# Norms handed over in steps, a first norm per token, and first weights in halves, in a two-layer diffusion backbone

## The chip, the core and the metric

The kernel runs on one core of a Trainium2 chip, as one program. What counts is the device time of an execution in microseconds (us); the profile is one execution. Engines: PE (TensorE, matmuls), DVE (VectorE), ACT (ScalarE), POOL (GpSimd), SP (its queue issues the DMAs here).

## The reference

Two layers work on 256 latent tokens and 256 context tokens of width 1024. Each layer is a half-step SwiGLU FFN, a token mixer (latent attention, pooling and gated linear attention) and a second FFN. Ahead of each of the three stands an RMS norm with a shift and a scale that come from a product of SiLU(c) with w_ada, nine vectors of 1024 a layer, other ones for latent and context tokens:

```
def rmsnorm(x, g):
    y = xf * lax.rsqrt(jnp.mean(xf * xf, axis=-1, keepdims=True) + EPS)
    return (y * g.astype(F32)).astype(x.dtype)
def modulate(x, shift, scale): return x * (1 + scale) + shift
def ffn_half_step(h, g, shift, scale, gate, w1, w3, w2):
    u = modulate(rmsnorm(h, g), shift, scale)
    return h + 0.5 * gate * ((jax.nn.silu(u @ w1) * (u @ w3)) @ w2)
...
    mod = (sc @ w_ada[l] + b_ada[l]).reshape(B, 1, N_MOD, D)
    h = ffn_half_step(h, g_ffn1[l], mod[:, :, 0], mod[:, :, 1], mod[:, :, 2], ...)
    u = modulate(rmsnorm(h, g_mix[l]), mod[:, :, 3], mod[:, :, 4])
    y, yc = token_mixer(u, uc, ...)
    h = h + mod[:, :, 5] * y
    h = ffn_half_step(h, g_ffn2[l], mod[:, :, 6], mod[:, :, 7], mod[:, :, 8], ...)
```

The context tokens go the same way until the mixer of the last layer.

## The kernel before

All activations lie turned, channels on the 128 partitions: h is 8 blocks (k = 0 to 7) of 128 channels by 512 tokens, the latent stream in columns 0 to 255 (stream 0), the context stream in 256 to 511 (stream 1). Every fp32 product is three fp32r products (`mm3`: whi·uhi, whi·ulo, wlo·uhi; lines 219, 220, 221). So each weight tile that a DMA brings to a `raw` buffer (four of them) is split by ACT (whi, L185) and DVE (wlo, L197), and each operand u as well (uhi on ACT, ulo on DVE, L475). `Weights` issues the loads on SP's queue in the order in which the program needs them, as far ahead as the raw buffers and a number of held tiles (`room`) allow. A scheduler sets the order on each engine from the program's order; each engine works its queue in order.

The modulation vectors come from w_ada in chunks of 512 columns. For chunks 0 to 3 of layer 0 (needed by the first norm; order 0, 2, 1, 3) and for two later ones PE makes the product (`ada`, L327), ACT copies it out (adaev), PE turns it (L339), and DVE adds up and adds the bias (mod, am). All other chunks are summed on DVE between other work (adaacc, L358).

The norm (`norm`): as each block of h is grown (h, L501), ACT squares it and DVE adds the square to acc (L448). When all eight blocks are in, PE multiplies acc with a matrix of 1/1024 (ms, L464), ACT makes rstd (Ln, Exp), DVE makes ut = h·am·rstd (L471), ACT uhi and DVE ulo. At the five places where one phase hands over to the next, called H1 (first FFN to mixer, layer 0), H2 (mixer 0 to the second FFN), H3 (to layer 1), H4 (first FFN to mixer, layer 1) and H5 (mixer 1 to the last FFN) below, all this stands between the last product of one phase and the first of the next. The last products are those of blocks 6 and 7, stream by stream: in the FFN `down([6, 7])`, in the mixer `out([6, 7], True)` with the blocks interleaved. The first product of a phase (`dense`) takes stream 0 over all k first and then stream 1. At H2 a chunk of the modulation for layer 0 (`ada_edge`) stands on PE between the norm and the first product.

The start: SP loads the first weights (512 KB), then x and ctx (8 x 256 KB), chunks 0 and 2 (8 x 256 KB each), three weights, chunks 1 and 3. PE turns x into h (32 transposes of 128x128, L283), and 16 squares, 14 additions and two means follow. `dense_first` computes the first six outputs (w1 and w3 of units m = 0, 1, 2) with u as it comes, k = 1 to 6 in pieces of 256 columns; chunks 1 and 3 lie between them. The constants of the mixer are loaded from ACT's queue after that (`setup_rest`).

Of the kernel before, what the change touches and what calls it, by code (L numbers as in the profile page):

```python
# [38 lines left out]
NHALF, NSLOT, ROOM_FFN, ROOM_MIX, RAWS = 4, 71, 20, 20, 4  # L39
ROOM_0, ROOM_1, LAST = 8, 36, 4  # L40
S0, S1, S2 = 7, 3, 3
# [40 lines left out]
class Weights:  # L82
# [11 lines left out]
    def run_ahead(self):  # L94
        while not self.record:
            while self.loaded < len(self.seq) and len(self.raws) + self.held_raw < RAWS:
                t = self.raw.tile([P, 1024], F32, tag="raw", name="raw")
                self.seq[self.loaded][0](t)
                self.raws[self.loaded] = t
                self.loaded += 1  # L100
# [37 lines left out]
class Net:  # L138
    def __init__(self, nc, a, cst, msk, vecs, wa2, out, pools, w):
# [5 lines left out]
        self.have = set()  # L145
        self.after, self.owed, self.on_pe, self.edge = iter(()), 0, False, []
# [45 lines left out]
    def split(self, hi, lo, src, f32hi):  # L192
# [4 lines left out]
        self.nc.vector.tensor_tensor(out=lo, in0=src, in1=f32hi, op=ALU.subtract)  # L197
# [7 lines left out]
    def cols(self, src, k0, nk, c0, n=P):  # L205
# [7 lines left out]
        return self.w.get(load, m, lambda r, hi, lo: self.halves(r, hi, lo, m))  # L213

# [19 lines left out]
    def setup(self):  # L234
# [15 lines left out]
        for j in (0, 2, 1, 3):  # L250
            if j == 1:
                self.w.run_ahead()
            self.early[j] = [self.slot(name="ada") for _ in range(KD)]
            for k, t in enumerate(self.early[j]):
                nc.sync.dma_start(out=t, in_=self.a["w_ada"][0, k * P:(k + 1) * P, j * T:(j + 1) * T])
# [3 lines left out]
        self.h = one.tile([P, KD, T], F32, name="h")  # L259
        self.csil = one.tile([P, KD, 32], F32, name="csil")  # L260
# [18 lines left out]
        self.acc = self.slot(name="acc")  # L279
        for k in range(KD):  # L280
            ps = self.ps()
            for j in range(4):
                nc.tensor.transpose(ps[:, j * P:(j + 1) * P], xin[j][k // 4][:, (k % 4) * P:(k % 4 + 1) * P], self.ident)  # L283
            if k % 2:
                self.act(out=self.h[:, k, :], in_=ps, func=AF.Copy)
            else:
                nc.vector.tensor_copy(self.h[:, k, :], ps)
            for s in range(2):
                self.square(k, s)

    def setup_rest(self):
# [23 lines left out]
    def ada(self, l, j):  # L315
# [4 lines left out]
        if early or self.on_pe:  # L320
# [15 lines left out]
            yield  # L336
# [7 lines left out]
            if early:  # L344
                yield
            return
# [108 lines left out]
    def norm(self, l, i, n):  # L455
# [3 lines left out]
        u = [(self.slot(F32R, "uhi"), self.slot(F32R, "ulo")) for k in range(KD)]  # L459
        rstd = self.slot(name="rstd")  # L460
# [6 lines left out]
        def some(s, c, ks):  # L467
            for k in ks:
                assert {(l, i, k // 4), (l, i + 1, k // 4)} <= self.have
                t, (hi, lo) = self.half("ut"), u[k]  # L470
# [924 lines left out]
```

## Time and profile before

| | |
|---|---|
| median of 3 runs | 2154.8 us (2153.69 to 2155.99) |
| the profiled execution | 2152.27 us, span 2150.5 us, mean granted clock 0.983 |
| PE busy | 2084.2 us (97%), 11388 instructions |
| DVE busy | 1453.7 us (68%) |
| ACT busy | 882.3 us (41%) |
| DMA | 290.43 MB, mean 135 GB/s |

In the rows of a timeline stand the start and the duration in us, the engine and the line of the kernel, the operation, the tile written and the tiles read (buffer numbers left out), the shape and the count, and in brackets the idle time of that engine before it and what ended it. PE's records overlap, so the pace is read from start to start. An fp32 matmul appears as two records. PEclk is the granted clock of PE, 1.00 being full.

### The profile page before, as it was taken

To read this page: it belongs to the slowest core of one execution; us is meant where nothing else is said; L and a number is where in the kernel's file an instruction comes from. 1 tells how busy PE (TensorE), PEld (TensorE's weight loads), DVE (VectorE), ACT (ScalarE), POOL (GpSimd) and SP (SyncE) were. 2 spreads that over 40 slices of the span, in tenths; PEclk is the share of its full clock that TensorE was granted. 3 is DMA by queue.
4 is the path that set the end of the run, shared out by engine and by line. 5 is a ranking of instruction groups with operands and counts; after the bars stand their busy time and mean duration, and the time that the engine had idled before them with its cause. 6 is when DMAs were issued, how large, how long until landed. Compare 5 with 4: busy or idle time off the path is not lost.

```text
span 2150.5 us, 29894 instructions
## 1 busy us (share of the span) xinstructions
PE 2084.2 (97%) x11388; PEld 1752.5 (81%) x11388; DVE 1453.7 (68%) x2870; ACT 882.3 (41%) x1797; POOL 2.0 (0%) x10
## 2 busy tenths in 40 slices
PE   7999999898999999999999989999999998999999
PEld 4888778786777887888888888888888777998997
DVE  4577877867586665666876785767544687666564
ACT  5232223455344555433223342323343656665552
POOL 0000000000000000000000000000000000000000
PEclk9999999999999999999999999999999989999999
DMA  9355554514432223445555453546442332566663
GB/s 318 100 152 157 172 166 134 160 39 127 118 108 69 79 69 98 119 124 152 164 164 161 135 149 102 151 141 186 137 115 59 96 101 80 142 163 192 181 197 127
DMA packets 431071, 290.43 MB, mean 135 GB/s; under 512 B 16464, under 2 KB 386768, under 8 KB 430928
## 3 DMA queue, kind: packets, MB, share of 16 engines
q1 hardware_dynamic: 430016, 287.09, 46.6%
q8 instruction: 89, 1.46, 0.3%
q10 hardware_dynamic: 912, 1.44, 0.2%
q14 instruction: 54, 0.44, 0.1%
HBM read 287.44 MB, written 1.05 MB: 134 GB/s over the span
## 4 chain that ended last, share of the span: by engine, by line
PE 74%; DVE 11%; DMA 9%; ACT 3%; issue 2%; ACTq 0%; SPq 0%; DVEq 0%
PE ps L219 17%; PE ps L220 17%; PE ps L221 17%; DMA raw<-in_ffn_w_dram 9%; PE fill L219 4%; PE fill L221 4%; PE fill L220 4%; DVE wlo L197 4%; DVE adaacc L358 2%; ACT whi L185 2%; PE sc L1031 1%; PE av L1067 1%; PE ada L327 1%; PE pt L1049 1%; PE gv L219 1%
## 5 line engine op out<-in xcount | busy, mean ns | idle before, releaser
L197 DVE TENSOR_TENSOR wlo<-raw,whi 128x512 fp32r<-128x512 f32 (+3 forms) x912 | 531.3, 619 | 290.0 <-ACT whi L185 279.6
L185 ACT ACTIVATE whi<-raw 128x512 fp32r<-128x512 f32 (+3 forms) x912 | 471.9, 568 | 521.5 <-DMA raw<-in_ffn_w_dram 469.8
L219 PE MATMUL ps<-uhi,whi 128*128 128x512 f32 (+1 forms) x1620 | 564.3, 350 | 8.7 <-ACT uhi L185 5.1
L221 PE MATMUL ps<-uhi,wlo 128*128 128x512 f32 (+1 forms) x1620 | 561.8, 348 | 1.1 <-DVE wlo L197 1.1
L220 PE MATMUL ps<-ulo,whi 128*128 128x512 f32 (+1 forms) x1620 | 562.3, 348 | 0.0
L219 PEld LDWEIGHTS ps<-uhi,whi 128*128 128x128 f32 x1620 | 308.0, 191 | 53.7 <-ACT uhi L185 8.7
L221 PEld LDWEIGHTS ps<-uhi,wlo 128*128 128x128 f32 x1620 | 308.8, 191 | 41.3 <-DVE wlo L197 3.6
L220 PEld LDWEIGHTS ps<-ulo,whi 128*128 128x128 f32 x1620 | 309.3, 191 | 37.9 <-DVE ulo L475 0.6
L358 DVE SCALAR_TENSOR_TENSOR adaacc<-raw,csil,adaacc 128x512 f32<-128x512 f32 x420 | 294.6, 744 | 1.6 <-DMA raw<-in_w_ada_dram 0.8
L219 PE MATMUL ps<-hi,whi 128*128 128x512 f32 (+1 forms) x738 | 272.8, 371 | 6.9 <-DVE h L501 5.4
L221 PE MATMUL ps<-hi,wlo 128*128 128x512 f32 (+1 forms) x738 | 272.0, 369 | 0.2 <-DVE wlo L197 0.2
L220 PE MATMUL ps<-lo,whi 128*128 128x512 f32 (+1 forms) x738 | 271.5, 368 | 0.0
L219 PE MATMUL fill<-uhi,whi 128*128 128x512 f32 (+1 forms) x576 | 203.9, 354 | 0.0
L221 PE MATMUL fill<-uhi,wlo 128*128 128x512 f32 (+1 forms) x576 | 195.9, 340 | 0.0
L220 PE MATMUL fill<-ulo,whi 128*128 128x512 f32 (+1 forms) x576 | 195.4, 339 | 0.0
L219 PEld LDWEIGHTS ps<-hi,whi 128*128 128x128 f32 x738 | 141.2, 191 | 29.8 <-DVE h L501 5.8
L221 PEld LDWEIGHTS ps<-hi,wlo 128*128 128x128 f32 x738 | 141.2, 191 | 23.2 <-DVE wlo L197 0.6
L220 PEld LDWEIGHTS ps<-lo,whi 128*128 128x128 f32 x738 | 141.3, 192 | 22.4 <-DVE lo L197 0.2
L570 DVE TENSOR_TENSOR silu<-silu,ps 128x512 f32<-128x512 f32 (+1 forms) x88 | 54.2, 616 | 133.7 <-ACT silu L185 79.3
L185 ACT ACTIVATE silu<-ps 128x512 f32<-128x512 f32 (+1 forms) x88 | 47.4, 539 | 195.4 <-PE ps L221 195.1
L219 PEld LDWEIGHTS fill<-uhi,whi 128*128 128x128 f32 x576 | 109.3, 190 | 21.7 <-issue 10.6
L220 PEld LDWEIGHTS fill<-ulo,whi 128*128 128x128 f32 x576 | 109.4, 190 | 13.5 <-issue 2.4
(265 smaller groups left out, 2192.0 us busy)
## 6 DMA issues: line engine op xcount, KB each, us to landing
raw<-in_ffn_w_dram SPq DMA_DIRECT2D x198, 512.0 KB, 4.4
raw<-in_w_ada_dram SPq DMA_DIRECT2D x128, 512.0 KB, 3.8
raw<-in_w_in_dram SPq DMA_DIRECT2D x86, 512.0 KB, 4.4
raw<-in_ffn_w_dram SPq DMA_DIRECT2D x48, 384.0 KB, 3.9
raw<-in_ffn_w_dram SPq DMA_DIRECT2D x48, 320.0 KB, 3.2
raw<-in_w_branch_dram SPq DMA_DIRECT2D x48, 256.0 KB, 2.9
ada<-in_w_ada_dram SPq DMA_DIRECT2D x32, 256.0 KB, 5.4
raw<-in_w_out_dram SPq DMA_DIRECT2D x16, 512.0 KB, 5.0
```

What stands on the lines that cost most here:

```text
L185: i = self.nc.scalar.activation(**k)
L197: self.nc.vector.tensor_tensor(out=lo, in0=src, in1=f32hi, op=ALU.subtract)
L219: mm(out, wh, xh, start=start, stop=False)
L220: mm(out, wh, xl, start=False, stop=False)
L221: mm(out, wl, xh, start=False, stop=stop)
L327: nc.tensor.matmul(ps[32 * g:32 * g + 32, :], self.csil[:, k, :], r[i], start=(k < 4), stop=(k >= 4))
L358: nc.vector.scalar_tensor_tensor(out=acc[s], in0=r[i], scalar=c, in1=acc[s], op0=ALU.mult, op1=ALU.add)
L570: nc.vector.tensor_tensor(out=s[:, 0:n], in0=s[:, 0:n], in1=p3[:, 0:n], op=ALU.mult)
L1031: nc.tensor.matmul(sc[:, 0:nk], q[h][:, tt * P:(tt + 1) * P], keys[h][:, k0:T], start=True, stop=True)
L1049: nc.tensor.transpose(pt[:, (2 * x + j) * P:(2 * x + j + 1) * P], ps_[j][:, (kt + x) * P:(kt + x + 1) * P], self.ident)
L1067: nc.tensor.matmul(av[0][64 * x:64 * x + 64, s * NL:(s + 1) * NL], v[2 * s + kt][:, (h + x) * 64:(h + x) * 64 + 64], pts[x][kt // 2][:, (k ...
```

## The change

The first norm no longer goes through acc. ACT squares x as it lies (tokens on partitions) and sums along the row in the same pass; DVE scales x by the token's factor (xr), PE turns xr into hr (32 transposes), and `first_norm` makes u from hr with one ACT pass (scale and bias) and two DVE operations. h is turned from x separately (`residual`): blocks 0 to 3 by 16 transposes that PE does ahead of those of xr, with copies on DVE behind the last scaling, blocks 4 to 7 by 16 transposes between chunk 0 and chunk 2. The first weights come in halves of the contraction (`both`: k = 0 to 3 or 4 to 7 of w1 and of w3, two DMAs of 256 KB into one raw buffer). Nothing but x stands ahead of chunks 0 and 2 any more, then follow three halves, chunks 1 and 3, a fourth half, the constants of `setup_rest` (on SP's queue now), and the rest. `dense_first` works the half k = 0 to 3 for all outputs and then the other half, all with 512 columns. While the first two halves are split, the wlo of a half are held back until u has been issued (`seconds`).

At H1 to H4 the norm goes in steps. The mean of stream 0 is issued after block 6 of stream 1, ahead of block 7 of stream 1 (`norm_ahead`); u of stream 0 is issued after the last product, and the mean and u of stream 1 from within the next `dense`, after k = 1 of stream 0 (`then`). In the mixer the last two blocks go one after the other within a stream, as in `down` (`out_last`). rstd becomes a tile of its own, the u tiles are taken one by one, and the slots are 70 instead of 71.

```diff
@@ setup
+                self.w.run_ahead(3)
...
-        self.acc = self.slot(name="acc")
+        for j in range(4):
+            for c in range(2):
+                self.act(out=junk, in_=xin[j][c], func=AF.Square, accum_out=sums[:, 2 * j + c:2 * j + c + 1])
+            f = fac[:, j:j + 1]
+            nc.vector.tensor_tensor(out=f, in0=sums[:, 2 * j:2 * j + 1], in1=sums[:, 2 * j + 1:2 * j + 2], op=ALU.add)
+            self.act(out=f, in_=f, func=AF.Ln, scale=1.0 / D, bias=self.eps[:, 0:1])
+            self.act(out=f, in_=f, func=AF.Exp, scale=-0.5)
+            for c in range(2):
+                normed = nc.vector.tensor_scalar(out=xr[j][c], in0=xin[j][c], scalar1=f, scalar2=None, op0=ALU.mult)
+        self.residual(range(4), [normed])
         for k in range(KD):
+            t = self.slot(name="hr")
             if k % 2:
-                self.act(out=self.h[:, k, :], in_=ps, func=AF.Copy)
+                self.act(out=t, in_=self.turned(xr, k), func=AF.Copy)
             else:
-                nc.vector.tensor_copy(self.h[:, k, :], ps)
+                nc.vector.tensor_copy(t, self.turned(xr, k))
...
@@ norm
+        for s, c in enumerate(streams):
+            mean(c)
             yield u
+            some(s, c, range(KD))
+            yield u
+    def norm_ahead(self, l, i):
+        order = [(l, i) for l in range(DEPTH) for i in (0, 3, 6)]
+        self.ahead = self.norm(*order[order.index((l, i)) + 1], T)
+        next(self.ahead)
+    def norm_go(self, l, i, n):
+        norm = self.ahead
+        if norm is None:
+            norm = self.norm(l, i, n)
+            next(norm)
+        self.ahead = None
+        u = next(norm)
+        return u, lambda: [next(norm) for _ in range(2)] if n == T else None
+    def first_norm(self):
+        for ks in ([0], [1], [2, 3], range(4, KD)):
+            for k in ks:
...
+                    self.act(out=hi[:, c], in_=self.hr[k][:, c], func=AF.Identity, scale=a, bias=b)
+                    nc.vector.tensor_scalar(out=t, in0=self.hr[k][:, c], scalar1=a, scalar2=b, op0=ALU.mult, op1=ALU.add)
+                    nc.vector.tensor_tensor(out=lo[:, c], in0=t, in1=hi[:, c].bitcast(F32), op=ALU.subtract)
+            yield u
@@ dense
+                if then and s == 0 and k == 1:
+                    then()
@@ dense_first
+        for half, groups in ((0, (range(4), range(4, 6))), (1, (range(6),))):
             for g in groups:
+                for k in range(4 * half, 4 * half + 4):
+                    for j in g:
+                        self.mm3(out[j], units[half][j // 2].block(j % 2 * 4 + k % 4), x[k], k == 0, k == KD - 1)
@@ ffn, down
+                    if c.start and k == 6:
+                        self.norm_ahead(l, i)
                     self.grow(o[k], k, l, i + 2, c, half == 1)
@@ mixer
-        u = self.u = next(self.norm(l, 3, T))
+        self.u, rest = self.norm_go(l, 3, T)
+        def out_last(dcs):
+            for c in (slice(0, NL), slice(NL, T)):
+                for dc, unit, p in zip(dcs, us, o):
+                    for k in range(KD):
+                        self.mm3(p[:, c], unit.block(k), (m[k][0][:, c], m[k][1][:, c]), k == 0, k == KD - 1)
+                    if c.start and dc == dcs[0]:
+                        self.norm_ahead(l, 3)
                     self.grow(p, dc, l, 5, c, True)
```

What it moves, in rows of the order in which the built programs issue (row, line, operation, tile written and tiles read, shape, count). PE at the start, before (x_86 and x_87 are the last tile of tokens; adaev is a chunk copied out, ms the mean):

```order
9 L283 MATMUL ps<-cst_72,x_87 128x128 x4
10 L327 MATMUL ada<-ada,csil 32x512 x8
11 L339 MATMUL ada_298<-cst_72,adaev 128x128 x4
12 L464 MATMUL ms<-acc,cst_72 128x256 x2
13 L327 MATMUL ada<-ada,csil 32x512 x8
14 L339 MATMUL ada_342<-cst_72,adaev 128x128 x4
15 L219 MATMUL ps<-uhi,whi 128x512
```

And after, from the last tile of tokens to the first transposes of the second half of h:

```order
5 L325 MATMUL ps<-cst_72,x_86 128x128 x4
6 L325 MATMUL ps<-cst_72,xr 128x128 x32
7 L373 MATMUL ada<-ada,csil 32x512 x8
8 L386 MATMUL ada_327<-cst_72,adaev 128x128 x4
9 L325 MATMUL ps<-cst_72,x_75 128x128
```

The mean is gone from between the chunks; 32 transposes of xr stand ahead of chunk 0, and 16 of x (from row 9 on) ahead of chunk 2. PE at H2, before, from the last product of w_out (hi, lo) to the first of the FFN (uhi, ulo):

```order
3626 L219 MATMUL ps<-hi,whi 128x256
3627 L220 MATMUL ps<-lo,whi 128x256
3628 L221 MATMUL ps<-hi,wlo 128x256
3629 L464 MATMUL ms<-acc,cst_72 128x256 x2
3630 L380 MATMUL ada<-adapart,cst 128x32
3631 L327 MATMUL ada<-raw,csil 32x512 x8
3632 L219 MATMUL ps<-uhi,whi 128x256
```

And after:

```order
3529 L236 MATMUL ps<-hi,whi 128x256
3530 L237 MATMUL ps<-lo,whi 128x256
3531 L238 MATMUL ps<-hi,wlo 128x256
3532 L429 MATMUL ada<-adapart,cst 128x32
3533 L373 MATMUL ada<-raw,csil 32x512 x8
3534 L236 MATMUL ps<-uhi,whi 128x256 x4
3535 L237 MATMUL ps<-ulo,whi 128x256
```

Both means have left this place: that of stream 0 now stands 24 matmuls ahead of the chunk, that of stream 1 24 matmuls behind the first product. DVE at H4, before, from the last grown block (h) to the first u:

```order
1443 L501 SCALAR_TENSOR_TENSOR h<-ps,am_2_176,h 128x256
1444 L448 TENSOR_TENSOR acc<-acc,sq 128x256
1445 L501 SCALAR_TENSOR_TENSOR h<-ps,am_2_176,h 128x256
1446 L448 TENSOR_TENSOR acc<-acc,sq 128x256
1447 L471 SCALAR_TENSOR_TENSOR ut<-h,am_4_177,rstd 128x256 x3
1448 L475 SCALAR_TENSOR_TENSOR ulo<-ut,mod_169,uhi 128x256
```

And after:

```order
1469 L577 SCALAR_TENSOR_TENSOR h<-ps,am_2_178,h 128x256
1470 L497 TENSOR_TENSOR acc<-acc,sq 128x256
1471 L577 SCALAR_TENSOR_TENSOR h<-ps,am_2_178,h 128x256
1472 L522 SCALAR_TENSOR_TENSOR ut<-h,am_4_179,rstd 128x256 x2
1473 L497 TENSOR_TENSOR acc<-acc,sq 128x256
1474 L526 SCALAR_TENSOR_TENSOR ulo<-ut,mod_171,uhi 128x256
```

The first two ut have passed the last addition to acc, and stand behind the last h.

More of the change, by code (lines that the diff above doesn't have):

```diff
@@ L92, in __init__, with run_ahead @@
         self.raws, self.parts = {}, {}
-    def run_ahead(self):
+    def run_ahead(self, raws=RAWS):
         while not self.record:
-            while self.loaded < len(self.seq) and len(self.raws) + self.held_raw < RAWS:
+            while self.loaded < len(self.seq) and len(self.raws) + self.held_raw < raws:
                 t = self.raw.tile([P, 1024], F32, tag="raw", name="raw")
-                self.seq[self.loaded][0](t)
+                loads = self.seq[self.loaded][0](t)
+                if self.net.tc:
+                    for i in loads or ():
+                        self.net.behind(i, [self.net.last])
                 self.raws[self.loaded] = t
@@ L213, in cols, with both, load @@
         return self.w.get(load, m, lambda r, hi, lo: self.halves(r, hi, lo, m))
+    def both(self, srcs, k0, c0):
+        views = [s[k0 * P:(k0 + 4) * P, c0:c0 + P].rearrange("(k p) c -> p k c", p=P) for s in srcs]
+        def load(t):
+            return [self.nc.sync.dma_start(out=t[:, i * T:(i + 1) * T].rearrange("p (k c) -> p k c", k=4), in_=v)
+                    for i, v in enumerate(views)]
+        return self.w.get(load, 2 * T, lambda r, hi, lo: self.halves(r, hi, lo, 2 * T))
     def mm3(self, out, wts, x, start, stop):
@@ L345, in ada @@
                 yield
+                if j in (0, 2):
+                    yield
             return
@@ L458, in norm @@
         streams = [slice(s * NL, (s + 1) * NL) for s in range(n // NL)]
-        u = [(self.slot(F32R, "uhi"), self.slot(F32R, "ulo")) for k in range(KD)]
-        rstd = self.slot(name="rstd")
+        u = [None] * KD
+        rstd = self.rstd
         def mean(c):
@@ L547, in ffn, with rest @@
         ahead = 3 if begin else 2
-        norm = self.norm(l, i, n)
         if begin:
+            norm = self.first_norm()
             self.adas(5)
-            u = next(norm)
+            self.residual(range(4, KD))
+            self.xin = None
             self.adas(5)
-            self.w.room = ROOM_0
-            first = unit(0)
+            part = lambda half, ms: [self.both((w1, w3), 4 * half, m * P) for m in ms]
+            first = [], []
+            for m in (0, 1):
+                self.seconds = []
+                self.w.room = 4 * m + 4
+                first[0].extend(part(0, [m]))
+                u = next(norm)
+                for second in self.seconds:
+                    second()
+            self.seconds = None
             next(norm)
             self.w.room = ROOM_1
-            first += unit(1) + unit(2)
+            first[0].extend(part(0, [2]))
+            first[1].extend(part(1, [0]))
+            def rest():
+                self.adas(1)
+                next(norm)
+                self.w.room = ROOM_2
+                first[1].extend(part(1, [1, 2]))
         else:
```

118 lines of the change are left out of this document (66 added, 52 removed).

## The prediction

> **What bounds the kernel now.** I read the totals first, then TensorE's waits, then the timelines of PE, DVE and ACT at the places the waits point to. The first fence is the page's line of busy times and the first line of TensorE's waits (us in total, times, longest).
>
> ```profile
> PE 2084.2 (97%) x11388; PEld 1752.5 (81%) x11388; DVE 1453.7 (68%) x2870; ACT 882.3 (41%) x1797; POOL 2.0 (0%) x10
> ...
> PE ms L464 <- DVE acc L448: 14.8, 7, 4.3
> ```
>
> TensorE is busy 2084.2 of 2150.5 us, so about 66 us of idle time are all that a change of order can win, apart from time at half clock. The largest wait is the one the change is aimed at: the mean matmul (ms) waits for the sum of squares 7 times, 14.8 us. The next fence is TensorE's timeline over the start (start, duration, operation, then in brackets the idle time and what ended it).
>
> ```profile
> 6.74 5.52 PE L283 MATMUL ps<-cst,x 128*128 128x128 f32 x32
> 12.37 5.71 PE L327 MATMUL ada<-ada,csil 128*32 128x512 f32 x16
> 18.76 0.66 PE L339 MATMUL ada<-cst,adaev 128*128 128x128 f32 x4 [0.69 <-ACT adaev L185]
> 22.30 1.10 PE L464 MATMUL ms<-acc,cst 128*128 128x256 f32 x4 [2.88 <-DVE acc L448]
> 23.33 3.32 PE L327 MATMUL ada<-ada,csil 128*32 128x512 f32 x16
> ...
> 32.05 0.79 PE L219 MATMUL ps<-uhi,whi 128*128 128x512 f32 x1 [3.98 <-ACT uhi L185]
> ...
> 52.67 1.92 PE L327 MATMUL ada<-ada,csil 128*32 128x512 f32 x16
> ...
> 71.02 0.28 PE L220 MATMUL ps<-ulo,whi 128*128 128x256 f32 x1
> 71.26 0.40 PE L219 MATMUL ps<-uhi,whi 128*128 128x512 f32 x1
> ...
> 75.37 0.39 PE L219 MATMUL ps<-uhi,whi 128*128 128x512 f32 x1
> ```
>
> The first dense product starts at 32.05. At 71.26 its last eighteen matmuls begin, one for each unit and product of k=7, and the next unit begins at 75.37: the stage lasts 43.3 us. Eighteen in 4.11 us are 0.228 each at 512 columns; at 256 columns (two from 71.02 to 71.26) they follow each other by 0.12, so two halves cost 0.24.
>
> **The start, step by step.** The new path runs through ACT, DVE and PE in turn. The rows for its steps (L356 has minimum/median/maximum in ns; the row with 206 is a group with its mean in ns):
>
> ```profile
> 7.62 1.28 ACT L181 ACT_TABLE_LOAD   x1
> 588.59 0.77 ACT L185 ACTIVATE p<-sc,mx,scal 128x512 f32<-128x512 f32 x1
> 589.34 0.59 ACT L185 ACTIVATE gqk<-fill 128x512 f32<-128x512 f32 x1
> L185 ACT ACTIVATE orstd<-orstd 128x4 f32<-128x4 f32 x4 | 0.8, 206 | 0.1
> L356 DVE TENSOR_SCALAR adaacc<-raw,csil x60: 477/480/486, 93.9 to 1527.4; 128x512 f32<-128x512 f32 x60
> 11.30 2.48 DVE L287 COPY h<-ps 128x512 f32<-128x512 f32 x4 [4.02 <-PE ps L283]
> 29.90 0.16 DVE L404 SCALAR_TENSOR_TENSOR am<-mod,vec 128x8 f32<-128x8 f32 x1
> 37.52 1.89 DVE L197 TENSOR_TENSOR wlo<-raw,whi 128x512 fp32r<-128x512 f32 x3
> 31.09 1.31 ACT L185 ACTIVATE uhi<-ut,mod 128x256 fp32r<-128x256 f32 x3 [1.66 <-DVE ut L471]
> ```
>
> ACT can begin squaring after its table load, at 8.90. An ACT pass that also sums takes 0.75 from start to the next start (588.59 to 589.34), so eight are 6.0; the eight one-column Ln and Exp at 0.2 are 1.6, a hop to DVE and back 0.3: the last token factor is there at 16.8. DVE then scales the last two tiles (0.4 each) and, in its queue behind them, copies the first half of h (2.5), for which PE's second half of xr transposes waits on its PSUM tiles; with the last transposes 0.6 PE is free at 20.7. Chunk 0 of the modulation comes next: 1.9 at the price of 52.67, since its weights, which paced PE at 12.37 to 18.08, have long landed. Copy out and transposes 1.3 (the gap and row at 18.76), 23.9. Sixteen transposes of x for the second half of h: between 1.5 and 2.8 (5.52/32 each), taken 1.5, 25.4. Chunk 2: 1.9, 27.3; at 23.33 it ran without a DMA wait, and now it runs later while its loads were issued earlier. Out and transposed 1.3, three small DVE operations 0.6, two uhi 1.0: 30.2, and 0.5 more for a part at half clock. First dense product 30.7, against 32.05: only 1.3 us earlier, because a chain of ACT, DVE and PE takes the place of the chain that ended at the mean.
>
> The stage behind it: 144 matmuls at 0.228 are 32.8, and chunks 1 and 3 with their transposes 5.0, so 37.8. Before, the same work with 256-column pieces for k=1 to 6 is 6 x 3 x (2 x 0.228 + 12 x 0.12) = 34.1, plus 5.0, 39.1 of its 43.3; 4.2 went to half clock and to waits for u. Now the halves of u come from DVE: after the first uhi stand, up to the ulo of k=1, two ulo, two wlo, four ut and two ulo more (0.6 each for wlo by 37.52, 0.4 for the others), 4.4 us, against 2.5 of PE work on k=0, a wait of 1.9; with 0.7 of half clock 2.6. The stage ends at 30.7 + 37.8 + 2.6 = 71.1 instead of 75.4: **4.3 us won at the start**. Bounds: all links at half clock (first dense at 34.3, below) leave 0.7, one more wait of 1.9 makes it -1; squares at the price of a plain copy and no loss behind them give 7. The tables moved from ACT's queue to SP's (1.2 MB by their shapes) stand behind chunk 3 and ahead of two halves of weights needed only after 72 matmuls, 16 us into the stage: nothing. Weights in halves: the same bytes; nothing.
>
> **The hand-overs.** H2, mixer 0 to the second FFN, is the dearest. DVE's row, then PE's, then the clock in the window (PEclk is the third number from the end):
>
> ```profile
> 896.46 1.27 DVE L501 SCALAR_TENSOR_TENSOR h<-ps,mod,h 128x256 f32<-128x256 f32 x3 [3.31 <-PE ps L221]
> 896.50 0.28 PE L221 MATMUL ps<-hi,wlo 128*128 128x256 f32 x1
> 898.93 0.67 PE L464 MATMUL ms<-acc,cst 128*128 128x256 f32 x2 [2.15 <-DVE acc L448]
> 900.53 3.30 PE L327 MATMUL ada<-raw,csil 128*32 128x512 f32 x16
> 903.76 0.58 PE L219 MATMUL ps<-uhi,whi 128*128 128x256 f32 x1
> 902.00:904.00 2.00, 2.00 (x13) 0.34 (x6) 1.91 (x7) 1.99 (x4) 0.00 (x0) 0.50 0.22 56
> ```
>
> After the last w_out matmul (896.50) all growing, both sums and both means stand in a row, and the chunk that follows runs at half clock: 3.3 instead of 1.9. Now stream 0's mean is issued before the last quarter of w_out, and PE goes straight from it into that chunk: 896.62 + 0.3 for that mean + 0.2 + 1.9 = 899.0, with u of stream 0 made meanwhile (h 0.4, ut 0.4, uhi 0.5). Stream 1's mean costs 0.3 inside the dense product. Won: 903.76 - 899.3 = **4.5**. Between 2.5 (if the chunk's last weights land 2 us late: they are needed 4 us earlier than now) and 5.
>
> At the other three no chunk on PE covers u. Rows of H1 (421), H3 (1276) and H4 (1644), DVE's and then PE's first product:
>
> ```profile
> 420.96 0.48 DVE L501 SCALAR_TENSOR_TENSOR h<-ps,am,h 128x256 f32<-128x256 f32 x1 [0.44 <-PE ps L221]
> 422.80 1.28 DVE L471 SCALAR_TENSOR_TENSOR ut<-h,am,rstd 128x256 f32<-128x256 f32 x3 [0.39 <-ACT rstd L185]
> 424.19 0.74 PE L219 MATMUL ps<-uhi,whi 128*128 128x256 f32 x4 [0.96 <-ACT uhi L185]
> 1276.20 0.48 DVE L471 SCALAR_TENSOR_TENSOR ut<-h,am,rstd 128x256 f32<-128x256 f32 x1
> 1278.43 0.78 PE L219 MATMUL ps<-uhi,whi 128*128 128x256 f32 x2
> 1644.23 0.48 DVE L501 SCALAR_TENSOR_TENSOR h<-ps,am,h 128x256 f32<-128x256 f32 x1 [2.50 <-PE ps L221]
> 1645.81 1.27 DVE L471 SCALAR_TENSOR_TENSOR ut<-h,am,rstd 128x256 f32<-128x256 f32 x3
> 1646.89 0.74 PE L219 MATMUL ps<-uhi,whi 128*128 128x256 f32 x4 [0.17 <-ACT uhi L185]
> ```
>
> DVE's new order puts ut right behind the last h, but not ahead of it. From ut to the first product go 1.1 us (1645.81 to 1646.89). H4: h at 1644.23 + 0.3 for the early mean, ut 0.4 later, product at 1646.0, and 0.3 for the second mean: 0.6 won. H1: the copy of vec1 lies between, ut at 421.9, product at 423.0, with the second mean 0.9 won. H3: there DVE is behind with weights and modulation sums and the order gives it the same operations ahead of ut plus a small one: ut at 1276.35, product at 1277.45, 0.6 for a mean at half clock: 0.4 won. Together **1.9**, between 0 and 4 (ut first thing after PE stops). H5 is unchanged.
>
> **Sum.** 4.3 + 4.5 + 1.9 = 10.7. The profiled execution took 2152.27 (2150.5 span and 1.8 around it): 2141.6. It lies 2.5 below the median of the runs, 2154.8, so the time to expect is 2144. A difference of 0.2% (4.3 us) is about what can be told from none.
>
> **The rivals.** *The start at half clock.* If the sparse work from 9 to 19 us (only transposes) leaves PE at half clock, chunk 0 and chunk 2 cost 3.3 each and the sixteen transposes 2.8: 4.1 more, of which 0.5 is counted already; first dense at 34.3, and 0.7 is left of the start: 7.1 in all, 2147.7. What decides is whether transposes alone bring the clock up. Two answers on the transposes, from 9 to 10 and from 10 to 11 us (mean ns in the second number behind the bar):
>
> ```profile
> L283 PE MATMUL ps<-cst,x 128*128 128x128 f32 x7 | 1.6, 409 | 0.0
> L283 PE MATMUL ps<-cst,x 128*128 128x128 f32 x11 | 1.5, 292 | 0.0
> ```
>
> They get faster, 409 to 292 ns, after three microseconds in which nothing but transposes had run. That speaks against this rival, but in the new order they come in bursts with gaps. [...] Chance 0.15.
>
> *The hand-overs keep their length.* DVE takes h of the last block, then ut, in order; where it is late (H3) or H2's chunk waits for weights, only the start's 4.3 is left: 2150.5. For it speaks DVE's 68%; against it, that at H4 DVE had been idle 2.5 us when h came. Chance 0.09, half of it within 0.2%.
>
> *Slower: the early mean stalls PE.* It stands in PE's queue ahead of a whole block of 24 or 33 products, and waits for stream 0's sum on DVE. What such a wait costs shows here, a product held up by DVE, and the clock behind it:
>
> ```profile
> 410.02 0.58 PE L219 MATMUL ps<-hi,whi 128*128 128x256 f32 x1 [3.44 <-DVE h L501]
> 416.16 0.32 PE L220 MATMUL ps<-lo,whi 128*128 128x256 f32 x1
> 415.89 0.41 DVE L448 TENSOR_TENSOR acc<-acc,sq 128x256 f32<-128x256 f32 x1
> ```
>
> 3.4 us of wait, then 28 matmuls from 410.02 to 416.16, 0.22 apart instead of 0.12, 2.8 more: 6.2 a place. Two places eat the whole gain and more, four give 24.8 - 10.7 = 14 us more, 2169. The point: it decides where DVE finishes stream 0's sum more than 3 us behind the block k=6 of stream 1. At H1 the sum is done at 416.3, when that block (33 matmuls from 410.02, 28 of them by 416.16) runs to 416.8; at H4 the slack is over 2 us, at H2 about half a microsecond. Chance 0.11, of it 0.09 slower, 0.02 within 0.2%.
>
> **How the numbers follow.** Likeliest, both parts pay: 0.54, 2139.5 to 2148.5, predicted 2144. Half clock at the start 0.15 (2147.7), hand-overs unchanged 0.09 (2150.5), slower 0.11 (2156 to 2169); better than the bounds of the middle, with a start of 7 and hand-overs of 9, 0.08 (2139); no effect at all 0.03. Faster 0.54 + 0.15 + 0.05 + 0.08 = 0.82; within 0.2% 0.04 + 0.02 + 0.03 = 0.09; slower 0.09. A range from 2137 to 2151 leaves out the slower case, the lower half of the better one and the no-effect case: about 0.2.
>
> **What would show it.** Right: the first dense product at 30 to 31.5 and the next unit at 70 to 72; the early means at H1 to H4 without a wait; H2's chunk in 2 us directly behind w_out; TensorE's wait for acc down from 14.8 to under 4. Wrong: a first dense product after 33, or a wait over 1 us in front of an early mean; or a loss in the first FFN behind 75 us, where the order of weights and modulation sums on DVE also moves and where I forecast nothing.

## The result, and the profile after

The changed kernel took 2143.51 us (median of 4, 2142.09 to 2145.75) beside 2155.14 for the kernel before (2153.69 to 2155.99): ratio 0.9948, 95% interval 0.9930 to 0.9965, so 11.2 us faster. The forecast was 2144.0 in a range of 2137 to 2151. The profiled execution took 2143.83, its span is 2141.7, 8.8 less than the span before.

First the page's line of busy times and four lines of TensorE's waits (us in total, times, longest):

```profile
PE 2078.9 (97%) x11308; PEld 1745.6 (82%) x11308; DVE 1452.2 (68%) x2872; ACT 887.3 (41%) x1805; POOL 2.0 (0%) x10
...
PE ps L236 <- ACT uhi L188: 9.8, 4, 4.9
...
PE ps L236 <- DVE h L577: 6.0, 2, 3.4
PE ms L513 <- DVE acc L497: 4.5, 3, 2.7
PE ps L236 <- ACT whi L188: 3.4, 3, 1.9
```

The mean's wait for acc fell from 14.8 us to 4.5, and 2.7 of that is H5, which the change leaves alone. The wait for uhi (9.8) now stands at the head of the list: part of one wait has turned into another. TensorE's timeline of the start shows chunk 0, chunk 2, the first dense product, and the first product of unit m=3:

```profile
19.50 1.92 PE L373 MATMUL ada<-ada,csil 128*32 128x512 f32 x16
...
24.55 1.92 PE L373 MATMUL ada<-ada,csil 128*32 128x512 f32 x16
...
29.73 0.73 PE L236 MATMUL ps<-uhi,whi 128*128 128x512 f32 x2 [1.81 <-ACT uhi L188]
...
71.16 0.39 PE L236 MATMUL ps<-uhi,whi 128*128 128x512 f32 x1
```

Both chunks take 1.92, the price at full clock (the trace's record of the granted clock has 1.00 from 18.00 to 31.65; at half clock, 0.50, a chunk took 3.30 in the kernel before). The dense product starts at 29.73 instead of 32.05, and the stage ends at 71.16 instead of 75.37. H2 on TensorE, from the early mean over the last w_out matmul and the chunk to the first product of the FFN:

```profile
888.81 0.59 PE L513 MATMUL ms<-acc,cst 128*128 128x256 f32 x2
...
891.99 0.28 PE L238 MATMUL ps<-hi,wlo 128*128 128x256 f32 x1
892.11 0.31 PE L429 MATMUL ada<-adapart,cst 128*128 128x32 f32 x2
892.34 2.34 PE L373 MATMUL ada<-raw,csil 128*32 128x512 f32 x16
894.62 0.74 PE L236 MATMUL ps<-uhi,whi 128*128 128x256 f32 x4
```

No row has a bracket, so TensorE waits for nothing here. From the last w_out matmul to the first product go 2.63 us; before they were 7.26 (896.50 to 903.76). The first products of H1, H3 and H4, and of H3 also the early mean and the last product ahead (1264.23):

```profile
419.51 0.74 PE L236 MATMUL ps<-uhi,whi 128*128 128x256 f32 x4 [1.60 <-ACT uhi L188]
...
1259.90 0.67 PE L513 MATMUL ms<-acc,cst 128*128 128x256 f32 x2 [1.35 <-DVE acc L497]
...
1264.23 0.28 PE L238 MATMUL ps<-hi,wlo 128*128 128x256 f32 x1
...
1269.51 1.22 PE L236 MATMUL ps<-uhi,whi 128*128 128x256 f32 x4 [4.85 <-ACT uhi L188]
...
1637.60 0.74 PE L236 MATMUL ps<-uhi,whi 128*128 128x256 f32 x4 [1.51 <-ACT uhi L188]
```

H1 and H4 wait 1.6 and 1.5 us for u; H3 waits 4.85, and its first product then has the long duration of half clock (1.22 against 0.74; the record has 0.50 from 1267.3 to 1274.1).

To place every microsecond I cut the span at marks that each trace has: the first and last silu of each FFN on ACT, the first `msk` matmul of each mixer, and h of block 5 in w_out on DVE. A stage is the time between two marks. Each number below is a difference of start times. "Again" is a second execution of the changed kernel; "start", "hands" and "H2" are the experiments that follow. The kernel before was traced once, in an execution of 2152.27 us of the first group; in the groups of the last four columns its runs had medians of 2148 to 2149. So a difference of a few us between its column and one of these can belong to the execution.

| stage (us) | before | after | again | start | hands | H2 |
|---|---|---|---|---|---|---|
| start, to the first silu | 72.22 | 67.96 | 69.20 | 68.76 | 72.72 | 66.68 |
| first FFN, first to last silu | 282.94 | 283.79 | 279.61 | 278.82 | 283.17 | 279.00 |
| H1, to msk | 94.96 | 94.07 | 94.65 | 93.09 | 94.03 | 93.02 |
| mixer 0, to h of block 5 | 435.42 | 434.79 | 433.49 | 434.21 | 434.28 | 433.82 |
| H2, to the first silu | 40.73 | 36.68 | 36.25 | 39.33 | 36.25 | 36.38 |
| second FFN | 280.78 | 280.84 | 280.85 | 280.85 | 280.84 | 280.84 |
| H3, last silu to first silu | 95.72 | 96.12 | 95.79 | 95.07 | 96.68 | 95.17 |
| first FFN, layer 1 | 279.79 | 279.79 | 279.79 | 279.78 | 279.80 | 279.79 |
| H4, last silu to msk | 84.62 | 84.10 | 84.12 | 86.11 | 84.11 | 86.06 |
| rest of the span | 483.32 | 483.56 | 483.55 | 483.88 | 483.12 | 483.94 |

From before to after: start -4.26, first FFN +0.85, H1 -0.89, mixer -0.63, H2 -4.05, H3 +0.40, H4 -0.52, the rest +0.3: the 8.8 us of the two spans.

### The profile page after: what moved, and what is told of

Its sections match the earlier page's. It is cut to its first block, busy times and chain, and to the rows that moved or that the text cites. A ratio compares the mean times of both kernels' runs of the same rounds, so it can differ in the third digit from the quotient of the medians.

```text
span 2141.7 us, 29782 instructions
## 1 busy us (share of the span) xinstructions
PE 2078.9 (97%) x11308; PEld 1745.6 (82%) x11308; DVE 1452.2 (68%) x2872; ACT 887.3 (41%) x1805; POOL 2.0 (0%) x10
## 4 chain that ended last, share of the span: by engine, by line
PE 74%; DMA 10%; DVE 10%; ACT 4%; issue 2%; ACTq 0%; DVEq 0%; SPq 0%
PE ps L236 17%; PE ps L237 17%; PE ps L238 17%; DMA raw<-in_ffn_w_dram 8%; PE fill L236 4%; PE fill L238 4%; PE fill L237 4%; DVE wlo L200 4%; DVE adaacc L407 2%; ACT whi L188 2%; DMA raw<-in_w_in_dram 1%; PE sc L1138 1%; PE av L1174 1%; PE pt L1156 1%; PE gv L236 1%
## 5 line engine op out<-in xcount | busy, mean ns | idle before, releaser
L200 DVE TENSOR_TENSOR wlo<-raw,whi 128x512 fp32r<-128x512 f32 (+3 forms) x912 | 531.1, 618 | 289.0 <-ACT whi L188 280.3
L236 PE MATMUL ps<-uhi,whi 128*128 128x512 f32 (+1 forms) x1584 | 557.1, 354 | 12.7 <-ACT uhi L188 9.8
L237 PE MATMUL ps<-ulo,whi 128*128 128x512 f32 (+1 forms) x1584 | 556.0, 352 | 0.2 <-DVE ulo L565 0.2
L238 PE MATMUL ps<-uhi,wlo 128*128 128x512 f32 (+1 forms) x1584 | 555.0, 351 | 1.0 <-DVE wlo L200 1.0
L236 PEld LDWEIGHTS ps<-uhi,whi 128*128 128x128 f32 x1584 | 300.2, 190 | 57.8 <-ACT uhi L188 12.2
L238 PEld LDWEIGHTS ps<-uhi,wlo 128*128 128x128 f32 x1584 | 301.2, 190 | 43.0 <-DVE wlo L200 3.6
L237 PEld LDWEIGHTS ps<-ulo,whi 128*128 128x128 f32 x1584 | 301.7, 190 | 39.4 <-DVE ulo L565 0.6
L236 PEld LDWEIGHTS ps<-hi,whi 128*128 128x128 f32 x738 | 139.9, 190 | 31.5 <-DVE h L577 6.4
```

Of the source, the lines that this page charges most:

```text
L200: second = lambda: self.nc.vector.tensor_tensor(out=lo, in0=src, in1=f32hi, op=ALU.subtract)
L236: mm(out, wh, xh, start=start, stop=False)
L237: mm(out, wh, xl, start=False, stop=False)
L238: mm(out, wl, xh, start=False, stop=stop)
```

## The experiments

Each group ran on one chip, beside the kernel before. Microseconds against it are (1 - ratio) times its median in that group (2148.8, 2148.1 and 2148.0). The changed kernel measured in two of these ways: 11.2 us above, 12.0 us in the second group.

**The start alone, and the hand-overs alone.** Does the sum of the parts hold? The first kernel is the changed one with the hand-overs undone, the second the kernel before with the new hand-overs.

```
start alone:                       hand-overs alone:
-  self.norm_ahead(l, i)           +  norm in steps, norm_ahead, norm_go, then, out_last
-  u, later mean and u of stream 1    (first norm, weights and loads as before)
+  u and mean at once; w_out blocks interleaved
```

> The changed kernel with the four hand-overs as before the change (both means and all of u behind the last product, last two w_out blocks interleaved by k); only the start is new. Theory 1 (the parts add, each by its own place): first dense product at 29.7 us, unit m=3 at 71.1, so 4.3 us less than before there, and the whole time 4.3 less than before (ratio 0.998). Theory 2 (the start's gain is given back inside the first FFN, because the weights are no earlier and TensorE meets the same waits and a longer time at half clock): 3 us or less are left at 410 us and at the end (ratio 0.9986 or nearer 1). Hand-overs H1 to H4 as before: waits for acc of about 14.8 less the 2.9 of the start.

> The kernel before the change with the new hand-overs alone (means in steps, u of stream 1 inside the next product, last w_out blocks one after the other); the start is the old one, first dense product at 32.0. Theory 1: 6.4 us less than before (ratio 0.997), of it 4.5 at H2 (the modulation chunk on TensorE in 2 us instead of 3.3, directly behind w_out), 0.9 at H1, 0.4 at H3, 0.6 at H4. Theory 2 (hand-overs carry almost all): 8 us or more (0.9963).

Start alone: 2142.78, ratio 0.9973 (0.9962 to 0.9983), 5.8 us faster. Hand-overs alone: 2141.93, ratio 0.9969 (0.9957 to 0.9981), 6.7 faster. I had 4.3 and 6.4; both lie in the intervals, and their sum, 12.5, is the change's 11.2 to 12.0 within them. The parts add up. TensorE at H2, without the new steps and with them:

```profile
888.27 0.67 PE L513 MATMUL ms<-acc,cst 128*128 128x256 f32 x2 [2.15 <-DVE acc L497]
889.14 0.67 PE L513 MATMUL ms<-acc,cst 128*128 128x256 f32 x2 [0.20 <-DVE acc L497]
...
889.88 1.92 PE L373 MATMUL ada<-raw,csil 128*32 128x512 f32 x16
```

```profile
892.39 0.59 PE L466 MATMUL ms<-acc,cst 128*128 128x256 f32 x2
...
895.93 1.92 PE L329 MATMUL ada<-raw,csil 128*32 128x512 f32 x16
```

The wait of 2.15 for acc is what the steps remove. But the old order's chunk took 1.92 here and 3.30 in the profile before: 1.4 of the 4.05 us that H2 won between the first two traces was half clock that the old order does not always meet. Without it H2 is worth 39.33 - 36.25 = 3.1 us.

**H2 alone.** The changed start and steps at H2 only sizes H1, H3 and H4 by what is missing; the changed kernel ran beside it. The edit, shortened:

```
-  self.norm_ahead(l, i)                     # in the FFN
+  if i in (0, 3): next(norm), next(norm)    # H1, H3, H4: all of the norm at once
```

> The changed start and the steps at H2 alone; H1, H3 and H4 as before. My terms: start 4.3 + H2 4.5 = 8.8 below the kernel before, ratio 0.9959, 1.9 above the change; in the trace H2's chunk directly behind w_out and the first product 2.5 to 2.7 behind the last w_out product. Rival: the hand-overs' gain lies mostly at H1, H3 and H4 (less half clock behind them), then only 4.3 + 2.5 = 6.8, ratio 0.9968.

> The changed kernel once more, beside the others of this group, to size its parts on one chip and to see a second execution. If the parts add up as predicted (start 4.3, hand-overs 6.4), it stands 10.7 us, ratio 0.995, below the kernel before. On the first FFN (first dense product to the first product of block 6, stream 1, at H1; 377 us in the changed kernel's trace, 370 to 372 where the hand-overs were undone or h was turned later): if the difference belongs to the order of the code, it is 377 again here; if it belongs to one execution (when a weight lands, where a half-clock stretch falls), 370 to 374.

H2 alone: 2137.75, ratio 0.9951 (0.9937 to 0.9965), 10.5 us; the changed kernel: 2137.11, ratio 0.9944 (0.9932 to 0.9957), 12.0. So 1.5 us are left for the other three, where I had 1.9, but the intervals overlap by more than that, and the table does not bear it out: H4 is 1.9 us shorter with the steps, H3 0.6 and H1 1.6 longer, in all 0.3 longer. At the old H3 and H4 TensorE waits at the second mean:

```profile
1260.51 0.78 PE L513 MATMUL ms<-acc,cst 128*128 128x256 f32 x2 [4.36 <-DVE acc L497]
...
1628.17 0.67 PE L513 MATMUL ms<-acc,cst 128*128 128x256 f32 x2 [1.42 <-DVE acc L497]
```

At H4 that wait was followed by 3.4 us at half clock (the trace's record of the granted clock has half clock from 1629.6 to 1633.0); with the steps there is none. By my estimate such a stretch of 3.4 us costs up to 1.7 us of work, most of the 1.9: the granted clock is 0.50 in it, and in the kernel before the matmuls of 256 columns follow each other by 0.22 at half clock and by 0.12 at full. At H3 the wait of 4.36 became one of 4.20 for uhi in the second execution of the changed kernel.

The second execution also settles two points. First FFN: 279.6 against 283.8 in the first trace of the same code, so that difference is not the code's. TensorE's waits there, first trace and second:

```profile
288.49 0.50 PE L236 MATMUL ps<-uhi,whi 128*128 128x512 f32 x1 [0.98 <-ACT whi L188]
...
291.69 0.80 PE L236 MATMUL ps<-uhi,whi 128*128 128x512 f32 x1 [1.92 <-ACT whi L188]
```

```profile
288.57 0.50 PE L236 MATMUL ps<-uhi,whi 128*128 128x512 f32 x1 [1.30 <-ACT whi L188]
289.90 0.50 PE L238 MATMUL ps<-uhi,wlo 128*128 128x512 f32 x1 [0.59 <-DVE wlo L200]
```

Weights come late around 288 us, 2.9 against 1.9 us, and 6.8 against 3.4 us of half clock follow. The five other traces with the new start and the same plan of modulation sums (start alone, H2 alone and the next three experiments) show 277.7 to 280.3, the two with the old start 282.9 and 283.2. So the new start may win some 3 us more in this FFN than I counted. That is not shown: both traces with the old start are of long executions (2152.27 us, and 2146.76, the longest of that kernel's six), and no run tests why weights should come earlier.

The other point is the clock at the start. The transposes of xr from 16 to 17 us and from 18.4 to 19.4 us (count, then busy us and mean ns), first trace and second:

```profile
L325 PE MATMUL ps<-cst,xr 128*128 128x128 f32 x7 | 1.7, 418 | 0.0
...
L325 PE MATMUL ps<-cst,xr 128*128 128x128 f32 x11 | 1.4, 278 | 0.0
```

```profile
L325 PE MATMUL ps<-cst,xr 128*128 128x128 f32 x7 | 1.8, 426 | 0.7 <-DVE xr L309 0.7
...
L325 PE MATMUL ps<-cst,xr 128*128 128x128 f32 x7 | 1.7, 422 | 0.0
```

And windows of 2 us (after the window: its length, busy us and instructions of PE, PEld, DVE, ACT, POOL, then PEclk, DMA share, GB/s), first trace and second:

```profile
16.00:18.00 2.00, 2.00 (x11) 1.70 (x10) 2.00 (x5) 1.81 (x3) 0.00 (x0) 1.00 1.05 387
18.00:20.00 2.00, 2.00 (x22) 1.44 (x24) 2.00 (x5) 0.99 (x2) 0.00 (x0) 1.00 1.05 382
```

```profile
16.00:18.00 2.00, 2.00 (x11) 1.70 (x10) 2.00 (x5) 1.81 (x3) 0.00 (x0) 0.50 1.04 382
18.00:20.00 2.00, 2.00 (x11) 2.00 (x10) 2.00 (x4) 0.87 (x2) 0.00 (x0) 0.50 1.06 386
20.00:22.00 2.00, 2.00 (x18) 1.02 (x20) 1.53 (x3) 0.61 (x2) 0.00 (x0) 0.69 1.15 308
```

From 16 to 18 us both traces have 11 instructions of like length (418 and 426 ns), so both run at the half-clock pace, although the first window prints 1.00. That 1.00 is no measurement: the first trace's record of the clock begins at 18.00, with full clock, and what lies ahead of the record is printed as full. In the second trace the record begins at 10.98 with full clock, falls to half at 14.39 and is back at 21.22, behind 5.4 us of transposes without a gap. So in both executions most transposes of xr run at half clock; in the first the full clock comes 3.2 us earlier, and the first dense product at 29.73 instead of 31.33. Of these 1.6 us, 0.3 lie ahead of the last burst of transposes (15.34 and 15.62). The clock falls back in this way in three of the ten traces with this start, which are all but the kernel before, the hand-overs alone and the next experiment (the three are the second execution, start alone and the earlier u): there chunk 0 begins 4.9 to 5.4 us behind the start of that burst, in the other seven 4.2 to 4.3. The rival of the half clock is half true: it holds for most transposes of xr in both executions, but chunks 0 and 2 and the sixteen transposes of x between them ran at full clock (all but the first 0.2 us of chunk 0 in the second execution), and the price between executions is some 1.2 us and not 4.1.

**Turning h later.** All 32 transposes of x between chunks 0 and 2, so that nothing stands ahead of xr on PE.

```
-  self.residual(range(4), [normed])
-  self.residual(range(4, KD))
+  self.residual(range(KD))
```

> The changed kernel with all 32 transposes of x for h (and their copies) between modulation chunks 0 and 2, none ahead of those of xr. Theory 1 (the start is bound by the chain ACT squares, DVE scaling, DVE copies of h, TensorE, chunk 0): chunk 0 starts about 2.2 us earlier (17.3 instead of 19.5), chunk 2 about 1 us earlier, first dense product at 28.7, 1 us less in all. Rival (TensorE at half clock when it does only transposes of xr, with gaps, up to there): chunk 0 takes 3.3 instead of 1.9 us and the first dense product comes at 30 or later, no gain.

2137.29, ratio 0.9943 (0.9930 to 0.9956): the same as the change. Its start on TensorE, with one row of DVE:

```profile
12.59 6.63 PE L324 MATMUL ps<-cst,xr 128*128 128x128 f32 x32 [5.65 <-DVE xr L309]
...
17.48 2.48 DVE L318 COPY hr<-ps 128x512 f32<-128x512 f32 x4 [0.66 <-PE ps L324]
...
22.37 3.66 PE L324 MATMUL ps<-cst,x 128*128 128x128 f32 x32
...
31.14 0.73 PE L236 MATMUL ps<-uhi,whi 128*128 128x512 f32 x2 [1.81 <-ACT uhi L188]
```

PE idles 5.65 us for the first xr, and the transposes of xr end at 19.2 as in the change (19.5). They follow each other without a gap, at 0.21 us each until 18.3 and at 0.11 from there, the pace of the 32 of x at 22.37; this trace's record of the clock begins at 18.28, with full clock. So it is TensorE at half clock that paces them, and DVE, whose copies of h are out of the way, waits 0.66 us for it. Chunk 0 ran at full clock (1.92) all the same: the rival's outcome, no gain, came true, and its reason only for the transposes. The 16 that came off this path then cost 1.75 between the chunks (3.66 against 1.91 for the 16 that the change has there).

**u of the first two blocks earlier still.** u of k=0 and 1, stream 0, ahead of the last h on DVE.

```
-  some(s, c, range(KD))
+  some(s, c, range(2)); yield u     # for stream 0, called ahead of the last h
+  some(s, c, range(2, KD))
```

> The changed kernel, with u of blocks k=0 and 1 of stream 0 made ahead of the last grown block instead of behind it. If the 1.5 to 1.6 us that TensorE still waits for uhi at H1 and H4 (and 4.85 at H3) come from DVE's order (last h, then ut), as theory 1 says, they go: 1.5 less at H1 and at H4, 2 to 3 at H3, in all 5 us less than the changed kernel. Rival: these waits are the latency of the last block itself or DVE being behind with weights and modulation sums; then ut made earlier only pushes weight splits back, and the time stays within 1 us of the changed kernel.

2146.66, ratio 0.9988 (0.9978 to 0.9997): only 2.6 us faster than the kernel before, some 9 slower than the change. Against the second execution H2 grew by 2.4 (38.63), H3 by 1.9 (97.73) and H4 by 3.1 (87.18). TensorE at H2 (chunk) and H4:

```profile
889.87 1.91 PE L373 MATMUL ada<-raw,csil 128*32 128x512 f32 x12
...
895.63 1.05 PE L373 MATMUL ada<-raw,csil 128*32 128x512 f32 x4 [1.15 <-DMA raw<-in_w_ada_dram]
```

```profile
1641.08 0.39 PE L238 MATMUL ps<-uhi,wlo 128*128 128x256 f32 x1 [0.84 <-DVE wlo L200]
1642.69 0.74 PE L236 MATMUL ps<-uhi,whi 128*128 128x256 f32 x4 [0.88 <-ACT uhi L188]
1644.07 0.38 PE L237 MATMUL ps<-ulo,whi 128*128 128x256 f32 x1 [0.64 <-DVE ulo L526]
```

What moves ahead on DVE pushes something back: the chunk's last four matmuls wait for their load, and at H4 wlo, uhi and ulo are late in turn, with 3.4 us of half clock behind them. An earlier u alone is no gain while DVE has the same work to do.

**Two PSUM tiles for a block.** At H1 and H3 TensorE waits for h (6.0 us in two waits) ahead of block 6, stream 1.

```
-  o = {k: self.ps() for k in ks}
+  o = {(k, c.start): self.ps() for k in ks for c in spans}
```

> The change, with a PSUM tile of its own for each stream of blocks 6 and 7 in the FFN (before: one tile for both streams of a block). Theory: block 6 of stream 1 waits for h of block 6, stream 0 (3.40 at H1, 2.57 at H3) only since both lie in one tile; with two tiles that wait is gone, but DVE is as late as ever, so the early mean behind it waits instead (2 to 4 us at H1 and H3): no more than 2 us gained in all, 0 likeliest. Rival: the wait was the loss itself, and 6.0 of wait plus about 3 of half clock behind it are won: 9 us below the change.

2137.82, ratio 0.9949 (0.9936 to 0.9963): no gain. The early means at H1 and H3:

```profile
405.02 1.19 PE L513 MATMUL ms<-acc,cst 128*128 128x256 f32 x2 [5.37 <-DVE acc L497]
...
1253.86 1.19 PE L513 MATMUL ms<-acc,cst 128*128 128x256 f32 x2 [3.90 <-DVE acc L497]
```

The wait for h is gone and stands in front of the mean, as expected. DVE is late, and TensorE waits for the next of its results in its place.

**Taking the modulation sums off DVE there.** DVE's rows at H3 of the changed kernel say what it is late with:

```profile
1266.00 2.07 DVE L407 SCALAR_TENSOR_TENSOR adaacc<-raw,csil,adaacc 128x512 f32<-128x512 f32 x3
1267.98 0.48 DVE L577 SCALAR_TENSOR_TENSOR h<-ps,am,h 128x256 f32<-128x256 f32 x1
...
1268.45 0.46 DVE L522 SCALAR_TENSOR_TENSOR ut<-h,am,rstd 128x256 f32<-128x256 f32 x1
```

The last product of the FFN began at 1264.23, and its h is made at 1267.98, behind three modulation sums. Four kernels move such sums: to the units ahead ("quiet", both FFNs of layer 0), to layer 1 ("quiet1", second FFN only), and simply later ("quiet01", both FFNs), the last ("quiet01_sep") also with two PSUM tiles. From 20 us ahead of the last product of the FFN to 4 us behind it, DVE works 14 such sums at H3 in the change (second execution), and 9, 6 and 0 in the first three kernels; at H1 it works 8 in the change, and none in the first and the third kernel.

```
-  if len(ks) == 1:
+  if len(ks) == 1 and not (half and phase < 2 and ks[0] > 2):   # quiet1: phase == 1
       self.adas(ADA["down"][phase])
-  up=(1.5, 1.25, 1, 0)
+  up=(1.66, 1.4, 1, 0)                                          # the first kernel only
```

> The change, with the modulation sums kept off DVE while the last three single blocks of the first two FFNs' second half and blocks 6 and 7 are grown, and as many more sums per unit ahead (1.66 and 1.4 quarters a unit instead of 1.5 and 1.25). Theory: at H1 and H3 TensorE waits for h, acc and uhi because DVE works modulation sums of 0.67 each between (11 of them from 1252 to 1268); without them the waits of 3.40 (H1) and 2.57 + 1.35 + 4.85 (H3) fall by half or more, and 5 to 8 us are won on the change. Rival: the weights' own splits set DVE there, or the sums cost as much where they go (first FFN at 290 us: whi waits of 2.9 now): no gain, or 2 to 4 us lost.

> The change, with no modulation sums asked for while the last three single blocks of the second FFN of layer 0 are grown; nothing is raised elsewhere, so these sums come later, in layer 1. Theory: what holds TensorE at H3 (2.57 + 1.35 + 4.85 us) is DVE at work on modulation sums between h and acc, and layer 1's first FFN has room for them (its stage lasts 279.8 us in every run so far, without a wait): the stage of H3 (last silu to first silu, 96 us) becomes 90.5 and the time 5 below the change. Rival: the sums cost as much where they go (as in the run where they went into the units ahead, which took 5.1 us there): 0, at most 2 gained.

> As the run before, and the same at the end of the first FFN of layer 0. Theory: the stage of H1 falls from 94.5 to 87, as in the run with raised sums, now without a longer FFN ahead of it, and H3 by 5: 11 to 13 below the change, about 2125. Rival: DVE lacks the time in the mixer or in layer 1 instead, and the stage there grows by what is won: within 3 of the change.

> As the run before, with a PSUM tile of its own for each stream of blocks 6 and 7. Theory: alone this brought nothing, since the early mean then waited 5.37 and 3.90 us for acc; with DVE free of sums acc is in time, and the wait of block 6 for h (6.0 at H3 in the run with raised sums) goes: 2 to 6 below the run before. Rival: DVE is late with the weights' second parts too: 0.

| | median, us | ratio (95%) | first FFN | H1 | mixer 0 | second FFN | H3 | FFN, layer 1 |
|---|---|---|---|---|---|---|---|---|
| the change, again | 2137.11 | 0.9944 (0.9932 to 0.9957) | 279.61 | 94.65 | 433.49 | 280.85 | 95.79 | 279.79 |
| to the units ahead | 2141.24 | 0.9969 (0.9957 to 0.9981) | 289.41 | 86.69 | 435.04 | 285.94 | 90.33 | 279.79 |
| H3 only, to layer 1 | 2129.49 | 0.9918 (0.9905 to 0.9932) | 279.41 | 92.68 | 434.10 | 280.85 | 86.76 | 281.32 |
| both, later | 2128.45 | 0.9911 (0.9897 to 0.9926) | 279.67 | 87.14 | 441.19 | 280.85 | 86.17 | 280.59 |
| both, two tiles | 2131.05 | 0.9917 (0.9903 to 0.9931) | 276.55 | 86.64 | 442.38 | 280.85 | 86.17 | 280.51 |

At H1 and H3 the sums are the cause: without them the stage of H1 shrinks by 7.5 to 8.0, and that of H3 by 5.5, 9.0 and 9.6, the more the fewer are left there. What that is worth hangs on where they go. In the units ahead of H1 and H3 they cost 9.8 and 5.1, about all that this brings; where the sums of H1 come later, mixer 0 grows by 7.7, all of the 7.5 won at H1. It holds no more sums than the change's (54 in both), but they lie elsewhere in it, and this line of TensorE's waits shows what the change's mixer 0 does not have:

```profile
PE pt L1156 <- DVE p L1146: 5.9, 1, 5.9
```

TensorE's clock is at half from 571.0 to 577.8 us around that wait. That the moved sums delay p is likely and not tested. In layer 1 the sums of H3 alone (126 in its first FFN instead of 108) cost 1.5 of 9.0. Two PSUM tiles add nothing. H3 with its sums in layer 1, DVE's rows and TensorE's:

```profile
1252.04 0.48 DVE L577 SCALAR_TENSOR_TENSOR h<-ps,am,h 128x256 f32<-128x256 f32 x1 [2.71 <-PE ps L238]
1252.44 0.87 DVE L522 SCALAR_TENSOR_TENSOR ut<-h,am,rstd 128x256 f32<-128x256 f32 x2
```

```profile
1253.51 0.74 PE L236 MATMUL ps<-uhi,whi 128*128 128x256 f32 x4 [1.51 <-ACT uhi L188]
```

Now DVE waits for TensorE, h is followed at once by ut, and the wait of 4.85 is 1.51, the length that H1 and H4 have. No half clock is left from 1245 to 1305 us, where the changed kernel had 6.8 and 10.2. I had expected 5 us and got 5.6 by the ratios (0.9944 to 0.9918). With or without H1, these kernels beat both: 17.6 and 19.1 us under the kernel before. The change itself was not in this group; it is compared through the kernel before, and the intervals of the two ratios just touch for H3 alone and are apart for both FFNs.

## Why the prediction was right

**The signs.** The next unit came at 71.16 (70 to 72 on record), the first dense product at 29.73 and in the second execution at 31.33 (30 to 31.5), and H2's chunk took 2.28 and 1.86 us directly behind w_out (2). The early means were to have no wait, and one over 1 us was to speak against the prediction: at H3 it waited 1.35 in the first trace and not in the second. The wait for acc fell to 4.5 and 2.8, where I had under 4.

**The start, 4.3.** Right in size: 4.26 to the first silu, 4.21 to unit m=3. Over the ten traces with this start the first silu comes at 66.1 to 69.9, in the median 67.8, against 72.2 and 72.7 with the old one. Two steps were off and cancelled. The first dense product came at 29.73 and not at 30.7: the last token factor was ready at 15.4 and not at 16.8, and the way from there took 0.4 more. The stage behind it took 41.4 and not 40.4, with 3.4 us at half clock from 31.7 to 35.1, which cost up to 1.7 by the estimate above, where I had counted 0.7. In the second execution the first dense product was at 31.33, and the start won 3.0.

**H2, 4.5.** Right in its steps: the means and the wait are gone from behind w_out, and the first product came 2.6 us behind the last w_out matmul in the first trace and 2.2 in the second; the steps on record (0.12 to its end, 0.2, 1.9) add up to 2.2. The size depends on the execution: 4.05 and 4.5 us against the one trace before, 3.1 against the old order at full clock. The missed point is that the old order's half clock there (1.4) is not in every execution.

**H1, H3, H4: 0.9, 0.4, 0.6.** Against the trace before they measured 0.89, -0.40 and 0.52 in the first trace, 0.3, -0.1 and 0.5 in the second. Against the two traces with the new start and the old hand-over there (start alone, H2 alone), H4 is 2.0 shorter, but H1 is 1.0 to 1.6 and H3 0.6 to 1.1 longer. At the hand-over itself the steps did what I had added up, or more: from the start of the last product of the FFN to the first of the next phase TensorE takes 2.0 us at H1 (3.6 to 4.0 in the old order), 4.6 to 5.3 at H3 (5.9 to 7.7) and 1.8 at H4 (3.0). The step that failed at H1 and H3 is that I took the stretch ahead of it as unchanged: from the last silu to that last product H1 takes 65.8 and 66.4 (63.1 to 65.5 in the old order) and H3 65.8 and 66.1 (63.7 to 65.7). The early mean stands there with its waits, weights come some 0.6 us late there at H1 (0.2 or less in the old order), and half clock falls there (3.4 and 6.8 us of it at H1 in the two executions, and 3.4 to 6.8 in the old order); the runs do not separate these. At H3 the hand-over stays long because the last h is itself behind modulation sums on DVE: with 6 of the 14 sums left there it takes 1.8 us. That was the argument of the rival on unchanged hand-overs, and it holds there.

**The sum, 10.7.** The ratios say 11.2 and 12.0. That the sum came so near is in part luck: by the stages H1 and H3 brought nothing that repeats, and 3.3 us in the first FFN and 1.9 in mixer 0 of the second execution lie where I had forecast nothing. How much of these belongs to the change is open, since the one trace before is of an execution some 4 us longer than the median of the kernel before in the second execution's group (2152.27 and 2148.1).

**The rivals.** *Half clock at the start*: chunk 0 ran at full clock (1.92) behind nothing but transposes. The clock's record begins with full clock at 10.06 in the kernel before, behind 3.3 us of transposes without a gap, and at 18.00 in the first trace, behind 2.7 us; in the second it is back at full at 21.22, behind 5.4. But in bursts with gaps the clock fell back to half in three of ten traces, in the second execution for 6.8 us (14.39 to 21.22). *The early mean stalls PE*: in the first trace it waited 0.40 at H1 and 1.35 at H3, not 3, and in the second not at all. I had placed the deciding point at 3 us behind block 6; the h that block 6 itself waits for (3.40 at H1) comes first and gives DVE that time, as the run with two PSUM tiles shows, where the mean waits 5.37.

## What to carry to other kernels

A chain that crosses a phase boundary can be shortened by issuing its first steps before the last block and its last steps inside the next phase, but only as far as the engine that carries it is free: where that engine works through fillers, the order of the chain's own steps changes little, and moving the fillers gives more (here 5.6 us for one line). Fillers have to go where the stage is bound by something else; the table of stages, taken between marks that all traces share, shows whether a gain at one place was paid for at the next, if a stage that half clock can touch is read from more than one trace: the first FFN of one program took 283.8 and 279.6.

## What the runs showed of the hardware

In these traces half clock comes in stretches of 3.41 us or a multiple of it: added up over the first 430 us, the traces' records of the clock have 3.4, 6.8, 10.2, 13.7, 17.1 or 20.5 us of it, and the same program had 13.7 in one execution and 20.5 in another. Within a trace the stretches start a whole number of 3.413 us apart: in the kernel before at 23.71, 30.54, 296.78 and 409.42, that is 2, 80 and 113 such lengths behind the first, and in the first trace of the change at 31.65, 291.06 and 407.12, 76 and 110 lengths behind the first. An idle time of TensorE of 1.4 to 1.6 us was followed by such a stretch in some places (H4 in the kernel with H2 alone, 1.42) and by none in others (in the change H4, 1.51, and H1, 1.60). So two executions can differ by a few microseconds without any difference in the work: by my estimate the 6.8 us between 13.7 and 20.5 are, at a granted clock of 0.50, up to 3.4 us.
